# Attention's second stage in a hybrid decoder trunk: shares sent a step earlier, a merge over fewer steps, residual loads spread out, and a reordered end

## The chip, the cores and the metric

One NeuronCore of a Trainium2 chip runs the whole program. The metric is the device time of one execution in microseconds (us). Engines are named as in the profile: PE is TensorE's matmul, PEld its weight load, DVE is VectorE, ACT is ScalarE, POOL is GpSimd, SP is SyncE, which only issues DMAs here.

## The reference, cut to what matters

Two layers work on x of 1024 tokens by 1024 channels in float32: first a gated short convolution, then an attention layer. The change is in the attention layer:

```
h = rms_norm(x, attn_norm)
proj = h @ w_in                                 # q, k, v for 3 groups of 16 heads, and a gate z
for g, (window, dilation) in enumerate(((128, 1), (512, 4), (2048, 16))):
    q, k = rms_norm(...), rms_norm(...)
    out[g], lse[g] = dilated_group_attention(q, k, v, bias, window, dilation)
alpha = softmax(stack(lse), axis=0)             # a share for each of the 3 groups
o = sum(alpha * out)                            # merged per head and token
x = x + (o * silu(z)) @ w_out
```

## The kernel before, in words

Everything up to the projections q, k, v and z comes before the part that changes; it leaves q and k (`qkd`), v (`vd`), z (`zd`) and the residual stream (`x1d`) in HBM. The second stage of attention follows, from about 1626 us of the span to its end. The program fixes the order of every engine's instructions there by hand: PE, DVE, ACT, POOL and SP (the DMA queue) each run strictly in the order in which the code emits them.

**Units and steps.** The heads come in 8 pairs (`hp`, two heads side by side on 128 partitions) with 3 groups each. Groups 0 and 1 make 4 steps, group 2 makes 2, so a pair has 10 steps and the stage 80, numbered 0 to 79. A step's work is a dictionary from a lag to functions: what stands at lag n is emitted n steps after the step's own number. Lag 0 is A (L877): logits on PE, the row maximum on DVE (L899), the exponential on ACT (L902). Lag `LB` = 2 is B (L904): PE transposes the probabilities, DVE or ACT copies them out of PSUM. Lag `LC` = 4 is C (L913): PE multiplies with V, and `finish` (L935) copies a full bank into O on DVE. Within one step the lags are emitted in the order 0, 1, 4, 3, 5 to 14, 2 (L1143), then the products in `extra`, then the loads and splits in `begins`.

**The merge of a pair.** The maxima and sums of groups 0 and 1 are stored to `nld` by POOL (L947, L950) one step after the last step of their group. After the pair's last step `end` (number 10 hp + 9) come, at the lags of L1052: `store` at 1 reads them back as `ml` (POOL, L945); `weights` at 3 and `shares` at 4 compute the three shares in small tiles (DVE, one ACT exponential); `store_shares` at 4 writes them to `fd` (POOL, L980); `spread(w)` (L982) reads them back, broadcast over 64 partitions, in two DMAs of 256 KB for each w, into `fb`, a pool of two tiles; `scale(w)` (DVE, L988) multiplies O of group w; `add(w)` (POOL, L991) sums; `gate` at 12 (DVE, L994) multiplies with silu(z); `high` at 13 (ACT, L998) and `low` at 14 (DVE, L1001) split the result into two float32r parts, `y2`. The third share's `spread(0)` stands at lag 8, behind `scale(2)`, because its tile is the one that `scale(2)` frees.

**Beside it.** The output product is made in three rounds of two pairs, one (128 x 512) tile a step (`some`, L1096: 6 matmuls of 512 columns), from step 10(2r + 2) + `LD` on, `LD` = 14; `add_sums` (L1102) adds a finished tile to the residual `acc` on DVE at the start of the next step. Its weights are split on ACT and DVE four and three steps ahead. The residual tiles `acc` are read from `x1d` by 16 loads of 256 KB on SP, one a step from step 4 on (L1123). The last pair is merged without HBM: `wide` (L1003) widens the shares in SBUF, `spread_last` (L1014) transposes them into PSUM on PE, and `last` (L1023) does the rest half by half, between the last products. `sqacc` (L85) is a (128 x 1024) tile of an earlier stage that this stage doesn't use.

Of the kernel before, what the change touches and what calls it, by code (L numbers as in the profile page):

```python
# [19 lines left out]
P = 128  # L20
# [15 lines left out]
def trunk(ctx: ExitStack, tc: tile.TileContext, a, out):  # L36
# [776 lines left out]
    with tc.tile_pool(name="sp", bufs=3, space=PSUM) as sp, tc.tile_pool(name="ptp", bufs=2, space=PSUM) as ptp, \  # L813
# [37 lines left out]
        def attention(hp, g):  # L851
# [128 lines left out]
                nc.gpsimd.dma_start(fd[hp].rearrange("w s (i r) -> i w s r", r=8), u["fo"])  # L980

            def spread(w):  # L982
                fb = u["fb", w] = fbp.tile([P, S], F32, name="fb", tag="fb")
                for s, hs in enumerate((lo, up)):
                    nc.gpsimd.dma_start(fb[hs], fd[hp, w, s][None, :].to_broadcast([64, S]))

            def scale(w):
                nc.vector.tensor_tensor(O[hp, w], O[hp, w], u["fb", w], op=OP.mult)  # L988

            def add(w):  # L990
                nc.gpsimd.tensor_tensor(O[hp, 1], O[hp, 1], O[hp, w], op=OP.add)  # L991
# [22 lines left out]
            def spread_last(hf):  # L1014

                hs = slice(64 * hf, 64 * hf + 64)
                for w in (2, 1, 0):
                    fb = u["fb", w] = sp.tile([P, 4, P], F32, name="ps", tag="ps").rearrange("p a b -> p (a b)")
                    for r in range(8):
                        nc.tensor.transpose(fb.rearrange("p (i r) -> p r i", r=8)[:, r],  # L1020
                                            u["wide", w][hs, r * P:r * P + P], ident[hs, hs])

            def last(hf, i):  # L1023
                h, z = half(hf), SZ[hp][:, half(hf)]
                if i == 0:
                    for w in (2, 1, 0):
                        nc.vector.tensor_tensor(O[hp, w][:, h], O[hp, w][:, h], u["fb", w], op=OP.mult)
                elif i == 1:
                    for w in (2, 0):
                        nc.vector.tensor_tensor(O[hp, 1][:, h], O[hp, 1][:, h], O[hp, w][:, h], op=OP.add)  # L1030
                    nc.vector.tensor_tensor(z, O[hp, 1][:, h], z, op=OP.mult)
                    if hf == 0:
                        y2[hp] = [ap.tile([P, S], F32R, name="qk", tag="qk", bufs=6) for _ in range(2)]
                    nc.scalar.activation(y2[hp][0][:, h], z, AF.Copy)
                else:
                    nc.vector.tensor_tensor(y2[hp][1][:, h], z, y2[hp][0][:, h].bitcast(F32), op=OP.subtract)
# [5 lines left out]
                    st = make(js, not steps)  # L1042
                    steps.append({lag: [f] for lag, f in zip((0, LB, LC), st)})
            end = steps[-1]
            end.setdefault(1, []).append(store)
            if g == 2:
                if hp == HP - 1:
                    todo = [(LB, weights), (3, shares), (3, wide), (LC, lambda: spread_last(0)),
                            (LC, lambda: last(0, 0)), (LC, lambda: last(0, 1))]
                    ending.update(spread=spread_last, last=last)  # L1050
                else:
                    todo = [(3, weights), (LC, shares), (LC, store_shares), (LC, lambda: spread(2)),  # L1052
                            (LC, lambda: spread(1)), (8, lambda: scale(2)), (8, lambda: spread(0)),
                            (9, lambda: scale(1)), (9, lambda: add(2)), (11, lambda: scale(0)),
                            (11, lambda: add(0)), (12, gate), (13, high), (14, low)]
                for lag, f in todo:
                    end.setdefault(lag, []).append(f)
            return steps, prefetch

        LB, LC = 2, 4  # L1060
        LD = 14
        W, ending = {}, {}

        def dense(ps, kts, dt, hf, first, last):
# [55 lines left out]
        for un, (k, prefetch) in at.items():  # L1120
            when(max(0, k - 2), load_v, *un)
        for i, (dt, hf) in enumerate(tiles):
            when(4 + i, residual, dt, hf)  # L1123
        for r in range(3):
            k0 = at[2 * r + 2, 0][0] + LD
            k = k0
            for i, (dt, hf) in enumerate(tiles):
                late = k >= len(steps)
                name = "pd" if not late else ("pd", ("ps", "ps", "pt", "pt")[min(k - len(steps), 3)])[i % 2]
                extra.setdefault(k, []).append(lambda r=r, dt=dt, hf=hf, name=name:  # L1130
                                               some((2 * r, 2 * r + 1), dt, hf, name))
                k += i % 2 if late else 1
        for kt in range(KT):
            k = at[kt // 2 * 2 + 2, 0][0] + LD - 4 + kt % 2 if kt < 6 else len(steps) - 5 + kt % 2
            when(k - 4 - kt % 2, fetch, kt)
            when(k, split, kt)
            when(k + 1, split_low, kt)
        for f in begins.pop(-1):
            f()
        k = 0  # L1140
        while k < len(steps) + LC or any(x >= k for x in extra):
            add_sums()
            for lag in (0, 1, LC, 3, *range(LC + 1, 15), LB):  # L1143
                for f in steps[k - lag].get(lag, ()) if 0 <= k - lag < len(steps) else ():
                    f()
            for f in extra.get(k, ()):
                f()
            for f in begins.get(k, ()):
                f()
            k += 1  # L1150
# [94 lines left out]
```

## Time and profile before

| what | value |
|---|---|
| time before, median of 3 runs | 1992.55 us (1991.82 to 1994.5) |
| profiled execution: its own time | 1993.42 us |
| profiled execution: span of its instructions | 1991.5 us |
| PE busy | 1942.4 us, 98% of the span |
| DVE, ACT, POOL busy | 75%, 45%, 44% |
| mean granted TensorE clock | 0.994 of 2.4 GHz |

The profile lists single instructions with their start, length and the idle time of their engine just before them, and what ended that idle time. Busy PE time counts a matmul until its modelled end. A stretch's granted clock of 1.00 is 2.4 GHz, 0.50 is 1.2 GHz. "DMA share" is the mean busy share of the core's 16 DMA engines.

### The profile page before, as it was taken

The page shows a single profiled execution, that of the slowest core. Times are in us where ns is not written, and L with a number is a line of the kernel's source. Part 1 is how long each engine was busy: PE and PEld are TensorE (multiplying, and loading weights), DVE is VectorE, ACT ScalarE, POOL GpSimd, SP SyncE. Part 2 cuts the span into 40 slices and gives each one's busy share as a digit, 9 for nine tenths or more (in the row PEclk, how much of TensorE's full clock was granted, in tenths as well). Part 3 has the DMA queues.
Part 4 walks back from the last instruction along what each step waited for, and adds up shares of the span by engine and source line. Part 5 has one row for each costly group of instructions (what it writes and reads, how often), then busy time and mean ns, then how long its engine had stood idle before and what let it go on. Part 6 is the DMA issues. An engine that isn't in the chain of part 4 may idle for free.

```text
span 1991.5 us, 29494 instructions
## 1 busy us (share of the span) xinstructions
PE 1942.4 (98%) x10302; PEld 1579.2 (79%) x10302; DVE 1484.1 (75%) x2751; ACT 903.5 (45%) x2042; POOL 885.3 (44%) x800
## 2 busy tenths in 40 slices
PE   8999999999999999999999999999999998899998
PEld 6888888888887888788887888788888876677776
DVE  6866665666666555898888788878899856787886
ACT  6433333333335344534343434343443448777770
POOL 0356767667665112444455444544454442222330
PEclk9999999999999999999999999999999999999999
DMA  6313232232225565323333323332433278767752
GB/s 198 113 62 96 71 106 85 85 106 70 89 77 176 165 235 171 118 85 106 106 106 117 96 96 117 107 105 85 127 99 106 93 239 259 206 174 219 207 142 85
DMA packets 116805, 254.25 MB, mean 128 GB/s; under 512 B 15822, under 2 KB 22718, under 8 KB 116656
## 3 DMA queue, kind: packets, MB, share of 16 engines
q1 hardware_dynamic: 93024, 177.42, 28.4%
q0 software_dynamic: 23632, 74.95, 12.5%
q8 instruction: 81, 1.33, 0.3%
q14 instruction: 68, 0.56, 0.1%
HBM read 193.05 MB, written 67.64 MB: 131 GB/s over the span
## 4 chain that ended last, share of the span: by engine, by line
PE 77%; DVE 10%; issue 5%; DMA 4%; ACT 2%; POOL 1%; SPq 0%; DVEq 0%; POOLq 0%; ACTq 0%
PE pp L301 18%; PE pp L304 18%; PE pp L303 18%; PE pp L552 3%; PE pp L553 3%; PE pp L551 3%; DVE ws L165 2%; PE pt L909 2%; PE ps L891 2%; DMA nld<-nl 1%; DVE blkc L711 1%; PE pp L374 1%; PE pp L376 1%; PE pp L375 1%; PE po L928 1%
## 5 line engine op out<-in xcount | busy, mean ns | idle before, releaser
L165 DVE TENSOR_TENSOR ws<-wr,ws 128x512 fp32r<-128x512 f32 x284 | 265.3, 936 | 115.5 <-ACT ws L164 114.6
L164 ACT ACTIVATE ws<-wr 128x512 fp32r<-128x512 f32 x284 | 178.3, 629 | 360.4 <-PE pp L304 236.7
L276 POOL TENSOR_TENSOR sr<-wr 128x512 f32<-128x512 f32 x136 | 192.6, 1416 | 264.6 <-DMA wr<-in_conv_w_in 69.7
L164 ACT ACTIVATE ws<-sr 128x512 fp32r<-128x512 f32 x272 | 169.7, 629 | 285.5 <-PE pp L304 236.2
L165 DVE TENSOR_TENSOR ws<-sr,ws 128x512 fp32r<-128x512 f32 x272 | 227.6, 845 | 80.4 <-ACT ws L164 77.6
L313 DVE TENSOR_TENSOR f<-pp,f 128x512 f32<-128x512 f32 x204 | 139.5, 684 | 90.2 <-PE pp L304 83.3
L902 ACT ACTIVATE xs<-xs,nl 128x128 f32<-128x128 f32 (+1 forms) x384 | 167.9, 439 | 68.9 <-DVE nl L899 57.7
L309 ACT ACTIVATE f<-pp 128x512 f32<-128x512 f32 x228 | 132.7, 582 | 28.4 <-POOL blkc L683 14.5
L899 DVE CUSTOM_DVE_ANT_0 xs<-ps,bt 128x128 f32<-128x128 f32 (+1 forms) x384 | 110.9, 347 | 27.5 <-PE ps L891 16.3
L716 POOL DMA_DIRECT2D qkd<-blkc x96 | 68.1, 717 | 131.6 <-DVE blkc L711 123.0
L674 ACT ACTIVATE f<-f 128x512 f32<-128x512 f32 x96 | 60.7, 633 | 140.2 <-DVE f L313 103.1
L276 POOL TENSOR_TENSOR sr<-wr,sr 128x512 f32<-128x512 f32 x68 | 88.9, 1307 | 65.7 <-issue 43.4
L301 PE MATMUL pp<-blkg,ws 128*128 128x512 f32 x272 | 107.3, 394 | 4.3 <-ACT f L309 4.2
L301 PE MATMUL pp<-blkf,ws 128*128 128x512 f32 x272 | 108.5, 399 | 0.7 <-ACT f L309 0.7
L301 PE MATMUL pp<-blka,ws 128*128 128x512 f32 x272 | 107.1, 394 | 0.7 <-ACT f L309 0.7
L301 PE MATMUL pp<-blkb,ws 128*128 128x512 f32 x272 | 107.4, 395 | 0.0
L301 PE MATMUL pp<-blkd,ws 128*128 128x512 f32 x272 | 107.0, 393 | 0.0
L304 PE MATMUL pp<-blkf,ws 128*128 128x512 f32 x272 | 106.3, 391 | 0.0
L304 PE MATMUL pp<-blkd,ws 128*128 128x512 f32 x272 | 106.0, 390 | 0.0
L304 PE MATMUL pp<-blka,ws 128*128 128x512 f32 x272 | 106.0, 390 | 0.0
L304 PE MATMUL pp<-blkb,ws 128*128 128x512 f32 x272 | 106.0, 390 | 0.0
L301 PE MATMUL pp<-blke,ws 128*128 128x512 f32 x272 | 106.0, 390 | 0.0
(329 smaller groups left out, 5388.0 us busy)
## 6 DMA issues: line engine op xcount, KB each, us to landing
wr<-in_conv_w_in SPq DMA_DIRECT2D x128, 256.0 KB, 3.0
wr<-in_wqk SPq DMA_DIRECT2D x96, 256.0 KB, 3.1
qkd<-blkc POOLq DMA_DIRECT2D x96, 256.0 KB, 3.1
qk<-qkd SPq DMA_DIRECT2D x48, 512.0 KB, 8.6
wr<-in_conv_w_out SPq DMA_DIRECT2D x64, 256.0 KB, 3.1
f<-in_x SPq DMA_DIRECT2D x48, 256.0 KB, 4.3
wr<-in_wv SPq DMA_DIRECT2D x48, 256.0 KB, 3.0
vd<-f POOLq DMA_DIRECT2D x48, 256.0 KB, 2.5
```

Source lines behind the costliest of these rows:

```text
L164: nc.scalar.activation(t[:, 0], src, AF.Copy)
L165: nc.vector.tensor_tensor(t[:, 1], src, t[:, 0].bitcast(F32), op=OP.subtract)
L276: nc.gpsimd.tensor_tensor(t, x, y, op=op)
L301: nc.tensor.matmul(ps, w[:, 0, ws], b[:, k, 0], start=new and k == 0, stop=False, skip_group_check=not new)
L303: nc.tensor.matmul(ps, w[:, 0, ws], b[:, k, 1], start=False, stop=False, skip_group_check=not new)
L304: nc.tensor.matmul(ps, w[:, 1, ws], b[:, k, 0], start=False, stop=end and k == 3, skip_group_check=not new)
L309: nc.scalar.activation(t, ps, AF.Copy)
L313: nc.vector.tensor_tensor(m, ps, m, op=OP.add)
L674: nc.scalar.activation(sq, t, AF.Square)
L716: nc.gpsimd.dma_start(qkd[hp, g, which].rearrange("p (c s) -> p c s", c=c) [:, :, hf * m:(hf + 1) * m], o.rearrange("p (c s) -> p c s", c=c))
L899: nc.vector.tensor_tensor_reduce(out=x, in0=ps[s][:, x0:x0 + nk].rearrange("p a b -> p (a b)"), in1=u["bt"][s][:, bs], op0=OP.add, op1=OP. ...
L902: nc.scalar.activation(x, x, AF.Exp, bias=nm, scale=-1.0, accum_out=L)
```

## The change

`spread(0)` writes into `sqacc` instead of a third tile from the pool of two, and with `store_shares` and the other two spreads it is emitted at lag 3, with `shares`; `store` of group 2 moves from lag 1 to 0, `weights` from 3 to 2 (at the end of that step), `scale(0)` and `add(0)` from 11 to 10, `high` from 13 to 12, `low` from 14 to 13. `LD` becomes 13, so every round of output products, and the splitting of its weights, starts one step earlier. The residual loads stand at every second step from 6 to 36. In the last pair, C of its last two steps comes one step earlier, B of the last step and `weights` move to the end of step 80, the steps behind it follow one step sooner, and the last products of the third round are spread over other PSUM banks and one step less.

```diff
--- before.py
+++ after.py
@@ -980,7 +980,7 @@
                 nc.gpsimd.dma_start(fd[hp].rearrange("w s (i r) -> i w s r", r=8), u["fo"])
 
             def spread(w):
-                fb = u["fb", w] = fbp.tile([P, S], F32, name="fb", tag="fb")
+                fb = u["fb", w] = fbp.tile([P, S], F32, name="fb", tag="fb") if w else sqacc
                 for s, hs in enumerate((lo, up)):
                     nc.gpsimd.dma_start(fb[hs], fd[hp, w, s][None, :].to_broadcast([64, S]))
 
@@ -1042,23 +1042,25 @@
                     st = make(js, not steps)
                     steps.append({lag: [f] for lag, f in zip((0, LB, LC), st)})
             end = steps[-1]
-            end.setdefault(1, []).append(store)
+            end.setdefault(0 if g == 2 else 1, []).append(store)
             if g == 2:
                 if hp == HP - 1:
-                    todo = [(LB, weights), (3, shares), (3, wide), (LC, lambda: spread_last(0)),
-                            (LC, lambda: last(0, 0)), (LC, lambda: last(0, 1))]
-                    ending.update(spread=spread_last, last=last)
+                    steps[-2][3] = steps[-2].pop(LC)
+                    end[3] = end.pop(LC)
+                    todo = [(2, shares), (2, wide), (3, lambda: spread_last(0)), (3, lambda: last(0, 0)),
+                            (3, lambda: last(0, 1))]
+                    ending.update(turn=end.pop(LB)[0], weights=weights, spread=spread_last, last=last)
                 else:
-                    todo = [(3, weights), (LC, shares), (LC, store_shares), (LC, lambda: spread(2)),
-                            (LC, lambda: spread(1)), (8, lambda: scale(2)), (8, lambda: spread(0)),
-                            (9, lambda: scale(1)), (9, lambda: add(2)), (11, lambda: scale(0)),
-                            (11, lambda: add(0)), (12, gate), (13, high), (14, low)]
+                    todo = [(LB, weights), (3, shares), (3, store_shares), (3, lambda: spread(2)),
+                            (3, lambda: spread(1)), (3, lambda: spread(0)), (8, lambda: scale(2)),
+                            (9, lambda: scale(1)), (9, lambda: add(2)), (10, lambda: scale(0)),
+                            (10, lambda: add(0)), (12, gate), (12, high), (13, low)]
                 for lag, f in todo:
                     end.setdefault(lag, []).append(f)
             return steps, prefetch
 
         LB, LC = 2, 4
-        LD = 14
+        LD = 13
         W, ending = {}, {}
 
         def dense(ps, kts, dt, hf, first, last):
@@ -1120,25 +1122,30 @@
         for un, (k, prefetch) in at.items():
             when(max(0, k - 2), load_v, *un)
         for i, (dt, hf) in enumerate(tiles):
-            when(4 + i, residual, dt, hf)
+            when(6 + 2 * i, residual, dt, hf)
         for r in range(3):
             k0 = at[2 * r + 2, 0][0] + LD
             k = k0
             for i, (dt, hf) in enumerate(tiles):
                 late = k >= len(steps)
-                name = "pd" if not late else ("pd", ("ps", "ps", "pt", "pt")[min(k - len(steps), 3)])[i % 2]
+                name = "pd" if not late else (("pd", "ps"), ("pd", "ps"), ("pd", "pt"), ("pt", "pd"))[
+                    min(k - len(steps), 3)][i % 2]
+                if i >= 14:
+                    name = "po"
                 extra.setdefault(k, []).append(lambda r=r, dt=dt, hf=hf, name=name:
                                                some((2 * r, 2 * r + 1), dt, hf, name))
-                k += i % 2 if late else 1
+                k += (i % 2 if i < 13 else 0) if late else 1
         for kt in range(KT):
             k = at[kt // 2 * 2 + 2, 0][0] + LD - 4 + kt % 2 if kt < 6 else len(steps) - 5 + kt % 2
             when(k - 4 - kt % 2, fetch, kt)
             when(k, split, kt)
             when(k + 1, split_low, kt)
+        when(len(steps), ending["turn"])
+        when(len(steps), ending["weights"])
         for f in begins.pop(-1):
             f()
         k = 0
-        while k < len(steps) + LC or any(x >= k for x in extra):
+        while k < len(steps) + LC - 1 or any(x >= k for x in extra):
             add_sums()
             for lag in (0, 1, LC, 3, *range(LC + 1, 15), LB):
                 for f in steps[k - lag].get(lag, ()) if 0 <= k - lag < len(steps) else ():
```

## Rows read from the trace of the kernel before

**Rows 1.** Busy times by stretch, one head pair each, the last from step 80 on.

```profile
core 0: us, PE busy (x) PEld busy (x) DVE busy (x) ACT busy (x) POOL busy (x), PEclk, DMA share, GB/s
1655.92:1692.25 36.33, 31.20 (x342) 24.46 (x340) 24.02 (x119) 29.32 (x119) 9.37 (x12) 0.91 0.92 280
1692.25:1729.59 37.34, 31.66 (x340) 24.00 (x338) 27.10 (x122) 28.94 (x113) 11.74 (x13) 0.94 0.73 196
1729.59:1770.11 40.52, 38.94 (x378) 29.77 (x378) 33.28 (x131) 32.16 (x120) 11.75 (x13) 0.97 0.81 230
...
1812.20:1853.02 40.82, 37.65 (x378) 28.60 (x377) 33.19 (x130) 31.20 (x116) 11.74 (x13) 1.00 0.73 191
...
1895.12:1934.98 39.86, 38.12 (x366) 29.45 (x362) 34.43 (x131) 31.17 (x110) 12.26 (x14) 0.96 0.55 158
1934.98:1991.50 56.52, 48.26 (x317) 38.39 (x316) 35.74 (x61) 7.67 (x18) 2.38 (x1) 0.97 0.21 76
```

**Rows 2.** Waits of the stage: engine, line, cause, us in total, times, longest.

```profile
DVE o L988 <- DMA fb<-fd: 16.4, 10, 4.1
...
DVE sz L994 <- POOL o L991: 5.1, 6, 1.9
```

**Rows 3.** Timeline of DVE, 1676 to 1698 us: start, us, what, idle before.

```profile
1683.87 1.23 DVE L988 TENSOR_TENSOR o<-o,fb 128x1024 f32<-128x1024 f32 x1 [4.08 <-DMA fb<-fd]
```

**Rows 4.** Timeline of PE, 1680 to 1697 us.

```profile
1685.99 2.07 PE L891 MATMUL ps<-qk 64*128 64x128 f32 x14 [3.90 <-DVE nl L899]
```

**Rows 5.** Busy times by stretch: after that idle time, columns as in Rows 1.

```profile
1684.50:1691.30 6.80, 5.18 (x32) 4.23 (x32) 6.23 (x36) 5.54 (x27) 4.95 (x5) 0.50 1.05 293
```

**Rows 6.** Timeline of POOL, 1785 to 1822 us, merge of the fifth pair.

```profile
1790.73 2.10 POOL L985 DMA_DIRECT2D fb<-fd  x4 [2.31 <-DMA fd<-fo]
...
1803.66 1.05 POOL L985 DMA_DIRECT2D fb<-fd  x2 [9.93 <-DVE o L988]
1804.69 1.56 POOL L950 DMA_DIRECT2D nld<-nl  x2
...
1817.14 0.57 POOL L945 DMA_DIRECT2D ml<-nld  x1 [7.53 <-DVE o L988]
1817.72 2.38 POOL L991 TENSOR_TENSOR o<-o 128x1024 f32<-128x1024 f32 x1
```

**Rows 7.** DMA issues of the whole run: count, KB each, median us to landing.

```profile
fb<-fd POOLq DMA_DIRECT2D x42, 256.0 KB, 8.3
...
acc<-x1d SPq DMA_DIRECT2D x16, 256.0 KB, 7.2
...
nld<-nl POOLq DMA_DIRECT2D x16, 8.0 KB, 10.2
...
fd<-fo POOLq DMA_DIRECT2D x7, 24.0 KB, 3.0
```

**Rows 8.** Timeline of DVE, 1810 to 1831 us, same merge.

```profile
1815.60 1.23 DVE L988 TENSOR_TENSOR o<-o,fb 128x1024 f32<-128x1024 f32 x1 [2.20 <-DMA fb<-fd]
...
1820.13 1.22 DVE L994 TENSOR_TENSOR sz<-o,sz 128x1024 f32<-128x1024 f32 x1 [0.72 <-POOL o L991]
```

**Rows 9.** Groups by line, 1640 to 1992 us: busy us, mean ns.

```profile
L939 DVE COPY o<-po 128x512 f32<-128x512 f32 x48 | 32.2, 685 | 1.1 <-PE po L922 0.4 <-PE po L928 0.3
```

**Rows 10.** Timeline of PE, 1949 to 1970 us, near the end.

```profile
1957.86 0.79 PE L1069 MATMUL pd<-y,y 128*128 128x512 f32 x1 [2.34 <-DVE acc L1105]
1958.45 0.63 PE L1070 MATMUL pd<-y,y 128*128 128x512 f32 x1
...
1960.99 0.39 PE L1070 MATMUL pt<-y,y 128*128 128x512 f32 x1
```

**Rows 11.** Timeline, 1586 to 1588.2 us, DVE beside POOL, an earlier stage.

```profile
1586.62 1.29 POOL L276 TENSOR_TENSOR sr<-wr 128x512 f32<-128x512 f32 x1 [2.48 <-DMA wr<-in_wz]
1586.74 1.26 DVE L65 TENSOR_TENSOR rit<-ri 128x64 f32<-128x64 f32 x1
```

**Rows 12.** Instructions of line 65: ns minimum, median, maximum.

```profile
L65 DVE TENSOR_TENSOR rit<-ri x72: 209/226/1341, 857.5 to 1586.7; 128x64 f32<-128x64 f32 x72
```

## Prediction

> **What bounds the kernel now.** I read the span cut by head pair first. Where output products run in most steps PE has next to no idle time; the loss sits elsewhere. Of the second pair's 36.33 us PE is busy 31.20, of the third's 37.34 it is busy 31.66, of the sixth's 40.82 it is busy 37.65, of the eighth's 39.86 it is busy 38.12, and of the end's 56.52 it is busy 48.26, part of the rest being the last adds and the stores behind the last matmul [rows 1]. Its granted clock is below 1.00 in four of these five as well, so some of the busy time is work at 1.2 GHz.
>
> The list of waits says why. DVE stands 16.4 us before `scale` for the broadcast shares, in ten waits of up to 4.1, and 5.1 us before `gate` for POOL's `add` [rows 2]. DVE's order is fixed, so the next step's row maxima stand behind such a wait: in the merge of the first pair DVE waits 4.08 us, and PE is idle 3.90 us for exactly those maxima [rows 3, 4]. After that idle time the granted clock is 0.50 (1.2 GHz) for 6.80 us, in which PE is busy 5.18 [rows 5]. At 2.4 GHz that work is 2.6 us, so 2.6 us is the clock's part.
>
> POOL's timeline of a merge shows two chains. The first four share loads are issued at 1790.73; the last two stand 9.93 us until `scale(2)` frees a tile and go out at 1803.66, and `scale(0)` waits 2.20 us for them [rows 6, 8]. Behind these two stand the stores of the next pair's maxima (1804.69); `ml` waits for their landing until 1817.14, `add(0)` stands behind `ml`, and `gate` waits 0.72 us for `add(0)` [rows 6, 8]. Seven merges go this way.
>
> **The change, part by part.** The sum is made against the profiled execution's own 1993.42 us (span 1991.5 and 1.9 around it), 0.87 over the median of 1992.55.
>
> *Shares a step earlier, the third with them.* No DMA and no instruction is added. `scale(2)` and `scale(1)` stay where they are, so their loads gain one step: 36.33/10 = 3.6 us in the second pair, 37.34/10 = 3.7 in the third [rows 1]. The largest wait, 4.08, leaves 0.5. The third pair of loads now goes out in the same burst, some four steps earlier, while `scale(0)` moves up by one, so its wait goes. The cost is a burst of six instead of four; two more loads are 0.52 MB, 1.8 us at the 293 GB/s that a full stretch moved [rows 5, 7], behind the others. POOL is passed by nothing but its own DMAs, and the maxima's stores no longer stand behind a wait.
>
> What can be won is bounded by the next engine. *Second pair:* PE's work at full clock is 31.20 - 2.6 = 28.6 us, ACT's 29.32. The DMA engines moved 280 GB/s, 10.2 MB; five residual loads of 256 KB fewer fall here, leaving 8.9 MB, 30.3 us at 293 GB/s. So at most 36.3 - 30.3 = 6.0. I take 4.5, since at such a share of the DMA engines the loads land late: lower end 1. *Third pair:* a clock of 0.94 means 4.5 us at half speed, so PE's work is 31.66 - 2.2 = 29.5 and the most is 7.8. Five residual loads are added, 7.3 + 1.3 MB, 29.4 us: the DMA engines come up to PE. I take 4.5, lower end 1. *Fourth pair:* 1.58 idle and 1.2 for the clock (0.97), most 2.8, taken 1.5. *Sixth:* 3.17 idle, taken 1.5. *Eighth:* 1.74 idle and 1.6 for the clock (0.96), most 3.3, taken 1.5 [rows 1]. About half, because there DVE is next: with `LD` one less the splits of two weight rows, `gate`, `weights` and `shares` fall on four neighbouring steps that have no output product to cover them. Lower ends 0. The fifth and seventh pairs have no PE idle time and give nothing.
>
> *`LD` = 13 and the residual loads.* The products move as a block; their number per round and the adds are the same. Cost nothing by themselves: PE has no idle time while they run. The 16 residual loads take no engine's time; they land in 7.2 us [rows 7] and the first is wanted 27 steps after it is issued. If their cover went, the price is the DMA time counted above.
>
> *The end.* The last product tiles wait 2.34 us for a bank whose add stands behind the merge of the first half on DVE, and then start at 1.2 GHz: 0.79 and 0.63 us a matmul where 0.39 is normal [rows 10]. A clock of 0.97 over 56.52 us is 3.4 us at half speed, 1.7 lost [rows 1]. The change gives the last tiles other banks and moves the merge up a step: most 4.0. It also puts C of steps 77 and 78 next to each other, and the second needs the bank that the first's copy (0.685 us [rows 9]) frees, behind a small `weights` on DVE: I take 1.2 for it and 0.3 for what is left of the wait, so 2.5 is won; lower end 0.
>
> *New costs.* `high` now stands in the same step as `gate` and ahead of ACT's copies of that step, so ACT stands until `gate` (1.22 us [rows 8]) is done; before, a step lay between. And `add(0)` on POOL (2.38 us [rows 6]) now runs while DVE reaches the split of a weight row in three merges. A DVE operation with both inputs in SBUF that meets a POOL operation ends with it: 1.26 us beside POOL's 1.29, where the median of that line is 0.226 [rows 11, 12]. Together they cost between 0 and 7.1 (three times 2.38); I take 2.0, because a step's maxima lie between `scale(0)` and the split and use up most of `add(0)`.
>
> The Trainium skill has this as a rule against the change (SBUF — State Buffer, "Who interferes with whom"): a VectorE operation with two SBUF inputs and a GpSimd operation that reads SBUF contend, and whoever comes second is blocked. The trace agrees, with the two rows just named. Taken at its full length three times it would make the sum 16.0 - 7.1 = 8.9 won instead of 14.0.
>
> *Sum:* 4.5 + 4.5 + 1.5 + 1.5 + 1.5 + 2.5 = 16.0, less 2.0: 14.0 us. 1993.42 - 14.0 = 1979.4 for an execution like the profiled one, 1978.6 beside the median; I say **1979.0**. The ends of the terms: 27.1 at most, and 2 less 7.1, a loss of 5, at the other end.
>
> **The rivals.** *More is won.* If the DMA engines keep up and the half-speed stretches all go, about 25 of the 27.1 us come: 1967.5. For it: each half-speed stretch in the stage stands behind idle time of the kind that the change removes [rows 4, 5]. Against it: the DMA share of the second pair is 0.92 [rows 1].
>
> *The DMA engines become the bound.* In 6.80 us of the first merge their share was 1.05 [rows 5]. If the six loads and the store of the shares (3.0 us [rows 7]) land as much later as they go out earlier, the second and third pairs give 1 each instead of 9, and 14 - 7 = 7 is left: 1985.5. For it: these are the pairs that lose most and have the fullest queues, and the third gets more loads. Against it: the second gets fewer.
>
> *Slower: one chain, stores of the maxima, `ml`, `add(0)`, `gate`, and now `high`.* The landing (10.2 us [rows 7]) holds `ml`, `ml` holds `add(0)` on POOL, `gate` waits on DVE, and with `high` behind it ACT now stands too. `gate` does not move up, but the steps before it get shorter. Priced at the longest wait of now, 1.9, and 1.22 for ACT, a merge loses 3.1, seven lose 21.8, against 16.0 won: 1992.55 + 5.8 = 1998.4. It decides above 2.3 us a merge. Against it: the stores are freed from the two loads ahead of them, which went out only at 1803.66 [rows 6].
>
> *It does not do what it says.* `ml` is emitted a step earlier, but its issue is held by the landing, not by its place. If `weights` now waits for it, the shares leave no sooner and only the third share's wait goes, which DVE loses again at `weights`: about 1992.
>
> **How the numbers follow.** A change of 0.2%, 4.0 us, is about what a measurement of this kernel can tell from none. Forecast 0.62 (its own range 1973 to 1985), more won 0.14, DMA engines 0.14, not as said 0.05, slower 0.05. The range 1969 to 1989 leaves out half of the second case and the last two: 0.17. Faster by more than 0.2%: the first three less a little for the third, 0.88; within 0.2%: 0.06; slower: 0.06.
>
> **What would show it.** Right: the second and third pairs take 31 to 33 us each, with a clock of at least 0.97; waits of `scale` for shares fall from 16.4 to under 4; no share load waits for `scale(2)`; the 2.34 us at the end shrinks to under 1 and a wait of about 1 appears before C of step 78. Wrong: waits before `gate` or `weights` in the place of those before `scale`; ACT idle between its exponentials and `high`; a DMA share near 1 with shares still landing late; or a gain in the fifth and seventh pairs, which I put at nothing.

## The result, and the profile after

The changed kernel takes 1983.18 us (median of 4 executions, 1981.16 to 1983.32) against 1992.44 us (4, 1991.82 to 1994.5) of the kernel before: 9.3 us won, ratio 0.9949 [0.9932, 0.9967]. Forecast was 1979.0, in a range of 1969 to 1989. The profiled execution after took 1981.16 us (span 1979.4), 2.0 under its median, and the one before 0.98 over its own. So the two traces differ by 12.1 us of span, of which some 3 us are scatter between executions; whatever is read from the traces alone adds up to 12.1, not 9.3. One execution in this document is an outlier, 4950.88 us in the last run (e11): its median below is that of all five, its ratio that of the other four.

The busy times by stretch of the changed kernel, one row for each head pair from the first, the last row from step 79 on, answer to [rows 1]:

```profile
core 0: us, PE busy (x) PEld busy (x) DVE busy (x) ACT busy (x) POOL busy (x), PEclk, DMA share, GB/s
1626.89:1654.91 28.02, 23.80 (x230) 17.02 (x230) 18.13 (x103) 25.87 (x101) 4.11 (x5) 1.00 0.71 250
1654.91:1686.66 31.75, 29.35 (x354) 23.04 (x351) 25.30 (x120) 29.52 (x121) 9.24 (x12) 1.00 0.90 250
1686.66:1722.71 36.05, 31.39 (x348) 23.72 (x348) 27.32 (x123) 30.22 (x116) 11.65 (x13) 1.00 0.88 233
1722.71:1764.95 42.24, 39.99 (x362) 30.69 (x364) 35.59 (x132) 31.03 (x115) 12.55 (x15) 0.92 0.94 275
1764.95:1806.44 41.49, 41.41 (x406) 31.94 (x402) 33.27 (x133) 28.77 (x112) 11.24 (x13) 1.00 0.70 208
1806.44:1846.58 40.14, 37.84 (x372) 28.90 (x374) 34.37 (x133) 31.64 (x119) 11.14 (x13) 1.00 0.72 191
1846.58:1888.07 41.49, 41.41 (x406) 31.94 (x402) 33.30 (x133) 28.78 (x113) 12.14 (x14) 1.00 0.71 204
1888.07:1924.72 36.65, 34.35 (x344) 26.30 (x345) 32.37 (x115) 29.78 (x102) 9.72 (x12) 1.00 0.52 150
1924.72:1979.40 54.68, 47.27 (x324) 38.33 (x323) 37.51 (x77) 9.42 (x27) 4.24 (x3) 1.00 0.21 78
```

[Rows 1] cut the end at step 80. The change reorders work inside step 79, so here both kernels are cut at its start. The same view of the kernel before, for the stretches that [rows 1] left out or cut otherwise:

```profile
1626.84:1655.92 29.08, 25.20 (x230) 18.22 (x230) 18.12 (x103) 26.11 (x101) 4.12 (x5) 0.94 0.78 266
1770.11:1812.20 42.09, 42.09 (x402) 32.49 (x400) 33.90 (x132) 29.38 (x114) 11.77 (x13) 1.00 0.72 202
1853.02:1895.12 42.10, 42.10 (x402) 32.50 (x401) 34.03 (x133) 29.39 (x114) 11.78 (x13) 1.00 0.70 191
1895.12:1932.92 37.80, 36.06 (x356) 28.01 (x352) 32.37 (x115) 29.45 (x101) 10.41 (x13) 0.95 0.58 166
1932.92:1991.50 58.58, 50.32 (x328) 39.83 (x326) 37.80 (x78) 9.39 (x27) 4.24 (x3) 0.97 0.20 73
```

The lengths can't be subtracted as they stand. `LD` = 13 moves the block of products by one step across the cuts, and a product tile has six matmuls that start 0.23 us apart, 1.4 us. Each of a round's two head pairs adds three matmuls to a tile. The same view for the first of the three counts the tiles (two such matmuls to a tile), after and then before, for pairs four and five:

```profile
1722.71:1764.95 42.24, 6.10 (x14) 2.64 (x14) 0.92 0.94 275
1764.95:1806.44 41.49, 7.85 (x18) 3.40 (x18) 1.00 0.70 208
```

```profile
1729.59:1770.11 40.52, 5.23 (x12) 2.27 (x12) 0.97 0.81 230
1770.11:1812.20 42.09, 8.72 (x20) 3.77 (x20) 1.00 0.72 202
```

One tile more in the fourth pair, one less in the fifth; likewise more in the sixth and eighth, less in the seventh and the end. With 1.4 us for it, the stretches changed by:

| stretch | before | after | change, tiles evened out | predicted |
|---|---|---|---|---|
| first pair | 29.08 | 28.02 | -1.1 | 0 |
| second | 36.33 | 31.75 | -4.6 | -4.5 |
| third | 37.34 | 36.05 | -1.3 | -4.5 |
| fourth | 40.52 | 42.24 | +0.3 | -1.5 |
| fifth and seventh | 42.1 each | 41.49 each | +0.8 each | 0 |
| sixth | 40.82 | 40.14 | -2.1 | -1.5 |
| eighth, to step 78 | 37.80 | 36.65 | -2.5 | -1.5 |
| from step 79 | 58.58 | 54.68 | -2.5 | -2.5 |

Most of what these changes add up to is work done at the higher clock: over these rows PE's busy time falls from 335.2 to 326.8 us for the same matmuls, its idle time only from 29.4 to 25.7. At a granted clock of 0.50 stood 23.9 us of the stage before (3.4 in the first pair, 6.8 in the second, 6.9 in the third, 3.4 each in the eighth and at the end), and 6.8 us after, all in the fourth pair.

The list of waits of the stage after has no row any more for `scale` behind a share (16.4 us in [rows 2]) nor for `gate` behind `add` (5.1 us). What DVE and ACT wait for in their place (us in total, times, longest):

```profile
ACT y L998 <- DVE sz L994: 4.9, 5, 2.1
...
ACT y L1082 <- DMA wraw<-in_wo: 2.6, 1, 2.6
DVE xs L899 <- DMA nld<-nl: 2.6, 1, 2.6
...
DVE mx L959 <- DMA ml<-nld: 2.2, 2, 1.7
```

[Rows 6] calls the merge that runs in the fifth pair's steps the fifth pair's; by the step of its loads (43) it is the fourth pair's. In POOL's timeline of the same merge after, six share loads go out in one go, with the store of the next maxima right behind them; the stand of 9.93 us of [rows 6] is gone:

```profile
1779.37 2.09 POOL L985 DMA_DIRECT2D fb<-fd  x4 [1.88 <-DMA fd<-fo]
1781.44 1.05 POOL L985 DMA_DIRECT2D sqacc<-fd  x2
1782.45 0.94 POOL L947 DMA_DIRECT2D nld<-nl  x1
```

The DMA issues of the stage after (count, KB each, median us to landing) show what the burst does to the landings; `fb` stood at 8.3 in [rows 7]:

```profile
fb<-fd POOLq DMA_DIRECT2D x28, 256.0 KB, 8.9
...
wraw<-in_wo SPq DMA_DIRECT2D x8, 512.0 KB, 17.4
...
sqacc<-fd POOLq DMA_DIRECT2D x14, 256.0 KB, 14.1
...
nld<-nl POOLq DMA_DIRECT2D x16, 8.0 KB, 8.7
...
nld<-nl POOLq DMA_DIRECT2D x8, 16.0 KB, 15.7
```

The 16 KB rows are the maxima and sums of group 0. They stand right behind the burst, which is six loads now and was four. Before, the same view had:

```profile
nld<-nl POOLq DMA_DIRECT2D x8, 16.0 KB, 11.1
```

Where the third pair ends, two of these late landings stop the engines in this execution. The store issued at 1704.79 lands 17.7 us later; the tile of maxima that it reads is one of three (`bufs=3` in `begin`) and is the one that step 30's row maxima write. DVE's timeline there, with a split that took 2.78 us where this line's median is 1.22, beside POOL's `add(0)` at 1724.16 (2.37 us):

```profile
1718.87 1.21 DVE L988 TENSOR_TENSOR o<-o,sqacc 128x1024 f32<-128x1024 f32 x1
1722.71 0.29 DVE L899 CUSTOM_DVE_ANT_0 xs<-ps,bt 128x128 f32<-128x128 f32 x1 [2.62 <-DMA nld<-nl]
...
1724.84 2.78 DVE L1085 TENSOR_TENSOR y<-wraw,y 128x1024 fp32r<-128x1024 f32 x1 [0.33 <-ACT y L1082]
```

ACT's timeline has the other: the weight row issued at 1703.59 landed at 1723.64, 20.1 us later.

```profile
1723.75 1.06 ACT L1082 ACTIVATE y<-wraw 128x1024 fp32r<-128x1024 f32 x1 [2.65 <-DMA wraw<-in_wo]
```

Behind these waits come two stretches of 3.4 us at a granted clock of 0.50, from 1723.5 and from 1733.7; they are the 0.92 of the fourth pair. Near the end PE's timeline has, in the place of 2.34 us and two slow matmuls [rows 10], three shorter stops at full clock. The first is the predicted wait for C of step 78; the third isn't new, it stood there with 1.15 us before the change as well:

```profile
1934.05 1.15 PE L922 MATMUL po<-pts,V 128*64 128x64 f32 x30 [0.69 <-DVE o L939]
...
1946.20 0.50 PE L1071 MATMUL pd<-y,y 128*128 128x512 f32 x1 [0.98 <-DVE acc L1107]
...
1957.20 0.50 PE L1072 MATMUL pt<-qk,y 128*128 128x512 f32 x1 [1.15 <-DVE qk L1036]
```

### The profile page after: what moved, and what is told of

It reads as the page before. It is cut to its first block, busy times and chain, and to the rows that moved or that the text cites. A ratio compares the mean times of both kernels' runs of the same rounds, so it can differ in the third digit from the quotient of the medians.

```text
span 1979.4 us, 29520 instructions
## 1 busy us (share of the span) xinstructions
PE 1934.5 (98%) x10302; PEld 1573.3 (79%) x10302; DVE 1486.2 (75%) x2751; ACT 902.5 (46%) x2042; POOL 882.9 (45%) x800
## 4 chain that ended last, share of the span: by engine, by line
PE 79%; DVE 12%; issue 4%; ACT 3%; DMA 1%; POOL 0%; SPq 0%; DVEq 0%; ACTq 0%; POOLq 0%
PE pp L301 18%; PE pp L304 18%; PE pp L303 18%; PE pp L551 3%; PE pp L553 3%; PE pp L552 3%; DVE ws L165 2%; PE pt L909 2%; PE ps L891 2%; PE po L928 2%; ACT xs L902 2%; DVE blkc L711 1%; PE pp L374 1%; PE pp L375 1%; PE pp L376 1%
## 5 line engine op out<-in xcount | busy, mean ns | idle before, releaser
L301 PE MATMUL pp<-blkb,ws 128*128 128x512 f32 x272 | 108.0, 397 | 0.0
L301 PE MATMUL pp<-blka,ws 128*128 128x512 f32 x272 | 107.1, 394 | 0.7 <-ACT f L309 0.7
L276 POOL TENSOR_TENSOR sr<-sr,wr 128x512 f32<-128x512 f32 x68 | 104.6, 1538 | 4.9
L304 PE MATMUL pp<-blkb,ws 128*128 128x512 f32 x272 | 106.7, 392 | 0.0
L303 PE MATMUL pp<-blkb,ws 128*128 128x512 f32 x272 | 106.5, 391 | 0.0
```

Of the source, the lines that this page charges most:

```text
L276: nc.gpsimd.tensor_tensor(t, x, y, op=op)
L301: nc.tensor.matmul(ps, w[:, 0, ws], b[:, k, 0], start=new and k == 0, stop=False, skip_group_check=not new)
L303: nc.tensor.matmul(ps, w[:, 0, ws], b[:, k, 1], start=False, stop=False, skip_group_check=not new)
L304: nc.tensor.matmul(ps, w[:, 1, ws], b[:, k, 0], start=False, stop=end and k == 3, skip_group_check=not new)
```

## The experiments

All times are medians, the ratios against the kernel before on the same chip (1992.1 to 1992.9 us there); e1 to e8, e10 and e11 start from the changed kernel. Lengths of pairs are those of one profiled execution each.

**The residual loads.** Put back to one a step:

```diff
-            when(6 + 2 * i, residual, dt, hf)
+            when(4 + i, residual, dt, hf)
```

> The changed kernel with the 16 residual loads back at one a step from step 4. Theory (late landings): the changed kernel gained only 1.3 us in the third pair and nothing in the fourth because DMAs land late there: a weight row in 20.1 us (ACT stands 2.65 us for it), the maxima's store in 17.7 us (DVE stands 2.62 us for its tile), and two half-speed stretches follow. With the residual loads early, both waits shrink by half or more and the third and fourth pairs get 2 to 4 us shorter, while steps 0 to 9 lose the 1.1 us and the second pair 1 to 2 us: in all -1 to +1 us against the changed kernel's 1983.2. Rival (the spreading itself is the gain of the first two pairs): the second pair loses 3 or more and the third wins nothing, 1986 or more.

1983.27 us, 0.9951 [0.9934, 0.9967]. The second pair takes 33.37 us (1.6 more), the third 34.40 (1.6 less), and the two waits of 2.6 us above are gone. In this execution the spread loads give in one pair what they take in the next; e10, which has the loads one a step too, takes 32.30 and 35.54 us there, so the sizes aren't settled.

**The tile of maxima.** Three more buffers:

```diff
-                u["nl"] = sm.tile([P, 8, 4], F32, name="nl", tag="nl", bufs=3)
+                u["nl"] = sm.tile([P, 8, 4], F32, name="nl", tag="nl", bufs=6)
```

> The changed kernel with six tiles instead of three for the maxima and sums (nl), so that no new unit waits for an old unit's store to land. Theory (two landings that hide one another): DVE's 2.62 us before step 30 go, but ACT stands for the weight row until about the same moment, so only 0 to 1 us is won: 1982.2 to 1983.2. Rival (DVE's wait alone is the stop): 2.6 us or more won, under 1980.6.

1982.37 us, 0.9953 [0.9935, 0.997]. By the busy times of its third and fourth pairs, the third is 3.4 us shorter than in the changed kernel, and the fourth has its full clock:

```profile
1687.18:1719.84 32.66, 29.11 (x338) 22.29 (x338) 27.20 (x123) 29.04 (x114) 11.67 (x13) 1.00 0.90 245
1719.84:1762.44 42.60, 38.58 (x371) 29.31 (x372) 35.27 (x132) 32.11 (x119) 12.56 (x15) 1.00 0.98 285
```

DVE's stop at that tile is gone, and it is gone in every run below with six tiles. But 3.4 us isn't shown to be its price, because other landings are late in other executions of the same steps. e7 has this run's program up to step 40, and its third pair takes 35.36 us, with `scale` waiting for shares again:

```profile
1714.78 1.22 DVE L988 TENSOR_TENSOR o<-o,fb 128x1024 f32<-128x1024 f32 x1 [0.82 <-DMA fb<-fd]
...
1723.55 1.22 DVE L988 TENSOR_TENSOR o<-o,sqacc 128x1024 f32<-128x1024 f32 x1 [1.57 <-DMA sqacc<-fd]
```

And with three tiles the stop shows up in the changed kernel's profiled execution only: e1, e3, e5 and e10 don't have it, and their third pairs take 34.3 to 35.5 us. The fourth pair stays long even at full clock, with a DMA share of 0.98; the medians (0.8 us apart) don't tell the two kernels apart.

**`high` behind the step's B.** ACT's copy then stands behind the evictions and isn't met by `gate`:

```diff
-                            (10, lambda: add(0)), (12, gate), (12, high), (13, low)]
+                            (10, lambda: add(0)), (12, gate), (15, high), (13, low)]
...
                 for f in steps[k - lag].get(lag, ()) if 0 <= k - lag < len(steps) else ():
                     f()
+            for f in steps[k - 12].get(15, ()) if 0 <= k - 12 < len(steps) else ():
+                f()
```

> The changed kernel with high emitted behind B's copies of the same step instead of ahead of them. Theory (ACT's stand behind gate costs, my step on new costs): ACT's 4.9 us of waits for gate go, PE's idle times of 1.55, 1.49 and 1.49 us before B in the fourth, sixth and eighth pairs shrink to under 0.7, and 2 to 3 us are won: 1980 to 1981. Rival (DVE's own work bounds these steps, 4.78 us busy of 4.85): PE idles as long, for DVE, and the time stays within 1 us of 1983.2.

1983.18 us, 0.9954 [0.9938, 0.997]. ACT's waits for `gate` are gone (in their place it waits 3.3 us in all for DVE's part of `weights`), and PE's idle time there, in the sixth pair, falls from 1.49 us to 0.55 and 0.37. Yet the sixth and eighth pairs take 40.13 and 36.67 us, as before the edit: ACT's stand costs nothing while DVE is the later of the two.

**Weight rows loaded sooner.** The six tiles of maxima, and two steps more for the loads:

```diff
-            when(k - 4 - kt % 2, fetch, kt)
+            when(k - (6 if kt < 6 else 4) - kt % 2, fetch, kt)
```

> Both landings taken out of the way: six nl tiles, and the weight rows of the first three rounds fetched two steps earlier. Theory (late landings): both waits of about 2.6 us before step 30 go, the half-speed stretch behind them too, and the third and fourth pairs together get 4 to 6 us shorter: 1977 to 1979. Rival (DVE's and ACT's own work bounds these steps): under 1.5 us won.

1985.53 us, 0.9963 [0.995, 0.9976]. It missed on all sides: the third pair takes 40.05 us, 4.0 more than in the changed kernel, clear of the 32.7 to 36.1 us of the other runs with this order. The weight rows land in time, but the query and key loads behind them don't, as PE's timeline shows:

```profile
1718.78 1.91 PE L909 MATMUL pt<-ident,xs 128*128 128x128 f32 x8 [1.07 <-DVE pts L847]
1725.70 1.65 PE L891 MATMUL ps<-qk 64*128 64x128 f32 x8 [5.02 <-DMA qk<-qkd]
```

**The end as before,** with `LD` = 13 kept:

```diff
-                    steps[-2][3] = steps[-2].pop(LC)
-                    end[3] = end.pop(LC)
-                    todo = [(2, shares), (2, wide), (3, lambda: spread_last(0)), (3, lambda: last(0, 0)),
-                            (3, lambda: last(0, 1))]
+                    todo = [(LB, weights), (3, shares), (3, wide), (LC, lambda: spread_last(0)),
+                            (LC, lambda: last(0, 0)), (LC, lambda: last(0, 1))]
...
-                k += (i % 2 if i < 13 else 0) if late else 1
+                k += i % 2 if late else 1
```

The banks of the last products (not shown) are as before too.

> The changed kernel with the end as before: the last pair's old lags, old banks and old spacing of the last products; LD stays 13. Measured on the stretch from step 79 to the end: 58.63 us before, 54.67 with the change, of which 1.4 is one product tile that LD moved out of it. Theory (my step on the end): the wait of about 2.3 us for a bank comes back and the stretch takes 56.5 to 57.5 us, 2 to 3 us longer than with the change. Rival (PE is bound there and only the granted clock differed): 54.7 to 55.5 at full clock.

1982.81 us, 0.9954 [0.9941, 0.9967], so undoing the end costs nothing that can be measured. Its end took 56.55 us in the profiled execution, 1.9 more than after, but with 3.4 us at half speed in it. In runs that keep the new end the same stretch takes 54.7 us without such a stretch (the changed kernel, e1, e2, e6, e7) and 56.2 to 56.4 with one (e3, e4, e8, e11). Like with like the reorder is worth about 0.3 us. The old end had the half-speed stretch in all four of its profiled executions (the kernel before, e5, e9, e10), the new one in four of nine; whether the reorder makes it rarer is open. In the place of the two bank waits of 0.69 and 0.98 us there is one, with `LD` = 13 already shorter than the 2.34 of [rows 10]:

```profile
1949.38 0.50 PE L1069 MATMUL pd<-y,y 128*128 128x512 f32 x1 [1.38 <-DVE acc L1105]
```

**The third share late again:** its own tile, its place and `scale(0)`, `add(0)` as before; the first two stay a step sooner.

```diff
-fb = u["fb", w] = fbp.tile([P, S], F32, name="fb", tag="fb") if w else sqacc
+fb = u["fb", w] = fbp.tile([P, S], F32, name="fb", tag="fb")
...
-(3, lambda: spread(1)), (3, lambda: spread(0)), (8, lambda: scale(2)),
+(3, lambda: spread(1)), (8, lambda: scale(2)), (8, lambda: spread(0)),
...
-(10, lambda: scale(0)),
-(10, lambda: add(0)),
+(11, lambda: scale(0)),
+(11, lambda: add(0)),
```

> The changed kernel with the third share as before: its own tile from the pool of two, spread(0) at lag 8 behind scale(2), scale(0) and add(0) at 11. The first two shares still go a step sooner. Theory (the third share is worth about as much as the step): scale(0) waits 0.5 to 2.5 us for its share again in most merges and gate waits for add(0), so the second, third, sixth and eighth pairs get 1 to 2 us longer; but the burst is four loads again, the maxima's store lands in about 11 us instead of 15 to 18, and the third pair loses its 2.62 us wait for it. In all +2 to +5 us: 1985 to 1988. Rival (the step alone is the gain, the third share is hidden either way): within 1 us of 1983.2 or faster, by the third pair's 2.62.

1992.76 us, 1.0003 [0.9991, 1.0014]: the whole gain is gone, more than was expected by any reading. Its list of waits has POOL's load issue behind `scale(2)` again and shares late again, although the first two are sent as early as in the changed kernel:

```profile
POOL fb L985 <- DVE o L988: 70.6, 5, 15.8
...
DVE o L988 <- DMA fb<-fd: 9.9, 5, 4.4
...
DVE sz L994 <- POOL o L991: 2.2, 2, 1.3
```

What stands behind that issue on POOL is late with it. In the merge of the fourth pair the stores of the next maxima go out at 1804.33, and `ml` only after their landing:

```profile
1803.30 1.04 POOL L985 DMA_DIRECT2D fb<-fd  x2 [15.77 <-DVE o L988]
1804.33 1.56 POOL L950 DMA_DIRECT2D nld<-nl  x2
...
1814.65 0.57 POOL L945 DMA_DIRECT2D ml<-nld  x1 [5.40 <-issue]
```

`weights` then waits for `ml`, and step 51, in which it stands, takes 7.5 us in place of 4.9. The loss isn't everywhere, though: the second pair takes 30.4 us here, less than in the changed kernel (some 1 us of it because `scale(0)` stands behind the cut), and the third 36.6. It is the fourth, sixth and eighth, with the splits of the weight rows, that lose 3.8 to 4.6 us each.

**The third share alone:** the kernel before with only this edit.

```diff
-fb = u["fb", w] = fbp.tile([P, S], F32, name="fb", tag="fb")
+fb = u["fb", w] = fbp.tile([P, S], F32, name="fb", tag="fb") if w else sqacc
...
-(LC, lambda: spread(1)), (8, lambda: scale(2)), (8, lambda: spread(0)),
+(LC, lambda: spread(1)), (LC, lambda: spread(0)), (8, lambda: scale(2)),
```

> The kernel before with one part of the change alone: spread(0) goes into sqacc and is emitted at lag 4 with the other two; nothing is moved a step earlier, scale(0) stays at 11. Theory (the third share's place is nearly the whole gain, as its removal from the changed kernel brought 1992.8): scale(0) waits no more, gate waits less, the second and third pairs keep their waits for the first shares (about 3 us together) and in all 5 to 8 us are won: 1984 to 1987. Rival (only the step and the third share together win, because the first shares' waits of 4.08 and 2.50 us take its place): 0 to 3 us won, 1989 to 1992.

1987.57 us, 0.9975 [0.9964, 0.9986]: 4.9 us (2.8 to 7.2 by the interval), about half of the gain, just under what was expected. The waits before `gate` are gone from its list, and those for shares fall from 16.4 us to:

```profile
DVE o L988 <- DMA fb<-fd: 6.8, 4, 2.4
```

By stretch it wins where e6 loses. The second pair gives only 0.9 us, the third 2.2, the fourth 2.4 (with the same number of product tiles as before), the sixth 2.8:

```profile
1657.61:1693.00 35.39, 31.70 (x358) 24.94 (x354) 23.93 (x119) 30.53 (x122) 9.32 (x12) 0.95 0.92 272
1693.00:1728.12 35.12, 31.09 (x339) 24.02 (x337) 27.00 (x123) 29.00 (x114) 11.64 (x13) 0.95 0.82 223
1728.12:1766.28 38.16, 37.08 (x368) 28.07 (x369) 33.08 (x131) 31.14 (x116) 11.65 (x13) 1.00 0.84 226
...
1808.01:1846.03 38.02, 37.15 (x378) 28.58 (x377) 33.11 (x131) 31.11 (x116) 11.08 (x12) 1.00 0.78 214
```

This profiled execution was one of its fastest (1984.91 of 1983.8 to 1991.54).

**The merge alone:** residual loads (as in e1) and the end (as in e5) undone together.

> The changed kernel with both the residual loads and the end as before, so that only the merge part and LD of 13 are left. Theory (the residual loads and the reordered end are worth nothing that shows): within 2 us of 1983.2. Rival (each hides the other's worth): 1986 or more.

1985.12 us, 0.9961 [0.9947, 0.9975]: 7.3 of the 9.3 us. With e1 and e5 this leaves some 2 us, which the intervals don't tell from nothing, for the other two parts together. What it has beyond e9 is the earlier step and `LD` = 13: 2.4 us by the medians, with intervals that overlap. In the profiled executions the stage, from the first pair's start to the end, takes 354.0 us here and 354.2 in e9. `LD` = 13 by itself was not tested.

**Splits away from `gate`.** Six tiles of maxima, and the weight rows of the second and third round loaded and split four steps sooner:

```diff
+            k -= 4 if kt in (2, 3, 4, 5) else 0
             when(k - 4 - kt % 2, fetch, kt)
             when(k, split, kt)
```

> The changed kernel with six nl tiles, and the weight rows of the second and third round fetched and split four steps earlier, in steps 45, 46, 65 and 66, where DVE is busy 2.3 to 2.5 us of 4.1 to 4.5. Theory (DVE's own work bounds the four steps without products in the sixth and eighth pairs, and POOL's add stretches a split there from 1.22 to 1.65 us): PE's 2.4 us of idle time in each of the two pairs fall under 1, the sixth and eighth pairs get 1 to 2 us shorter than 40.1 and 36.7, and the third pair stays at the 32.7 us that six tiles gave: 1976 to 1979 in all. Rival (ACT or the DMAs hold these steps as much as DVE): the two pairs stay within 0.5 us.

1979.59 us, 0.9944 [0.9932, 0.9957]. The sixth and eighth pairs take 38.96 and 35.50 us, 1.2 less each, well clear of scatter: 40.1 to 40.2 and 36.7 in all of the changed kernel, e1 to e5 and e10. The fifth and seventh take 42.05 each, 0.56 more. The rest of the expectation missed: PE's idle time in each of the two pairs is 1.4 us, not under 1, the third pair's 35.36 us are not 32.7, and the time is just above the range. The splits moved from pairs in which DVE is late to pairs in which PE is busy throughout: DVE's load about `gate`, and the lock of split and `add(0)` with it, were part of the sixth's and eighth's length.

**Both:** e7 with `high` behind B as in e3.

> As the run before, and high behind B's copies of its step. Theory (once DVE's splits are gone, ACT's stand behind gate is next): another 0.5 to 1 us less in each of the fourth, sixth and eighth pairs, 1974 to 1978 in all. Rival (gate's place on DVE is what B waits for, whichever engine copies): no difference to the run before.

1979.24 us, 0.9937 [0.9923, 0.995], the shortest of all, but above the expected 1974 to 1978; its interval overlaps that of the changed kernel. With DVE relieved, `high`'s place now is worth 0.5 us in the sixth and eighth pairs, and nothing in the fourth (43.65 us, ACT waiting 2.58 for the weight row):

```profile
1806.45:1844.86 38.41, 37.39 (x371) 28.94 (x373) 31.71 (x130) 30.02 (x117) 11.98 (x14) 1.00 0.76 212
...
1886.91:1921.87 34.96, 33.94 (x344) 26.33 (x345) 29.71 (x113) 28.20 (x101) 9.70 (x12) 1.00 0.44 126
```

**Residual loads with a hole,** on e8, so that none falls into the merge that runs in the third pair's steps:

```diff
-            when(6 + 2 * i, residual, dt, hf)
+            when(4 + 2 * i if i < 8 else 23 + i, residual, dt, hf)
```

> Run e8 (six nl tiles, four weight rows split earlier, high behind B's copies) with no residual load in steps 19 to 30: eight at every second step from 4 to 18, eight from step 31 to 38. Theory (the DMA engines are what still holds the third pair and the head of the fourth: ACT stands 2.58 us for a weight row there): that wait falls under 1, no share lands late, the third pair takes 31.5 to 33 us and the fourth 41 to 42, 1975 to 1977 in all. Rival (the queue of six share loads alone delays the weight row): the two pairs stay at 33.6 and 43.7 us, 1979.

1981.13 us, 0.9942 [0.9927, 0.9956]. The weight row's wait is gone and the fourth pair is 41.63 us, but the third is 35.05 (33.59 in e8): `scale(0)` now waits 1.68 us for its share and `weights` 1.52 us for `ml`. Another landing is late, and no time is won. That the hole made it late isn't shown: e7 waits as long for its shares without it.

## Why the prediction was right, and where not

**The mechanism held.** No share load waits for `scale(2)`, the waits for shares and before `gate` went to nothing in this profile (in the other runs with this order up to 2.9 us for shares are left in all, and at most 2.1 in one wait), and the second pair's 31.75 us are the 31 to 33 forecast, at full clock: 4.6 us against 4.5. The sixth pair gave 2.1 against 1.5. The eighth gave 2.5 against 1.5, part of it the half-speed stretch that stood behind its clock of 0.96 [rows 1]. Some 0.8 us of either only crossed a cut, as said below. That POOL's in-order queue was the lever is shown by e6 and e9: without the third share's early place nothing is left; with it alone, about half. The second pair is the exception: its gain is the earlier step, as the sum had it, since it is there without the third share's place (30.4 us in e6) and hardly there with that alone (35.39 in e9). The rest of the merge's 7.3 us, as far as the medians show it, takes the earlier step and `LD` = 13 as well.

**The step that failed is "third pair 4.5, fourth 1.5".** They gave 1.3, and lost 0.3. I took the burst of six as 1.8 us more DMA time behind the four loads and said that the stores of the maxima no longer stand behind a wait. They don't, but one of them stands behind the burst: 17.7 us to landing. I named `ml` as who waits for them, and not the row maxima three units on, which reuse the tile that the store reads. With six tiles that stop is gone, and in e2 the third pair is 32.66 us, inside the forecast. But four runs with three tiles don't have the stop either, and in e7, with six, late shares make the pair 35.36. So the error is wider than one tile: at the end of the third pair something lands 1 to 3 us late, now the store, now a share, now the weight row on SP's queue (ACT's 2.65 us in the fourth pair, with half-speed stretches behind it), and which one differs between executions. e4 and e11 moved loads, and each time another wait stood in the place of the one removed. That is the rival "the DMA engines become the bound" at work in these two pairs, not as a share of 1 throughout, but as landings of 15 to 20 us. The burst by itself isn't enough for it: e9 has the same burst a step later, with the product rounds a step later as well, and wins 4.6 us in these two pairs; the profiled executions with the new order give 1.0 (the changed kernel) to 4.0 (e2) in the two together, against 6.0 forecast, but for e4, which loses. What makes the difference to e9 stays open. I also counted five residual loads into the third pair and not the four that fall into the fourth; e1 and e10, without those four, take 42.55 and 40.71 us there, so nothing shows them to be the cause.

**The end** came out at 2.5 us as forecast, for other reasons. e5 puts the reorder at about 0.3; the clock is 1.5 to 1.7 by the lengths above, and the remaining 0.6 or so is in e5 as well, so it came with `LD` or the merge. The predicted wait before C of step 78 came at 0.69 us (1.2 forecast), and the 2.34 us became 0.98, but they became 1.38 without the reorder too. The step that failed here is "the change gives the last tiles other banks and moves the merge up a step" as the source of the 2.5.

**The new costs** were sized well and placed partly wrong. The lock of [rows 11] came at each of the three splits: 2.78, 1.65 and 1.65 us in place of 1.22, 2.4 us in all where I took 2.0 with ACT's part. The Trainium skill's rule (SBUF — State Buffer, "Who interferes with whom": whichever of the two comes second is blocked) agrees with these rows. The 7.1 us of the prediction were not reached, since the split met only the tail of `add(0)` twice. ACT's stand before `high` was there (four times 0.6 to 0.8 us, and 2.1 in the last pair's steps), and e3 shows that it cost nothing by itself.

**Put at nothing:** the residual loads, rightly as far as e1's median shows; the fifth and seventh pairs lost 0.8 each, which I had excluded. In e6, with `LD` = 13 as well, both take 40.70 us, just one tile less than before, and in e9, with the third share's place but `scale(0)` at lag 11, 41.73 and 42.09 us, nothing more than before. So the 0.8 come with `scale(0)` at lag 10. They aren't time lost but work that crosses the cut: the changed kernel's DVE timeline has that `scale(0)` (1.22 us) at 1805.31, in step 49 and ahead of the sixth pair's first row maximum at 1806.44; in e6 it stands behind the cut. Taken in twos, fifth and sixth gave 1.3 us, seventh and eighth 1.7, against 1.5 each forecast. The first pair's 1.1 us is clock alone, and luck: 28.0 us in the changed kernel, e1, e2 and e6, 29.1 in the kernel before and all other runs, which have 3.4 us at half speed there.

**The other rivals.** The slower chain through `ml`, `add(0)` and `gate` didn't form: `weights` waited 2.2 us for `ml` in all and `gate` not at all. "More is won" failed at the third and fourth pairs. Its argument, that each half-speed stretch stands behind idle time that the change removes, does not hold for the first pair and the end, where the same stops are there with and without such a stretch.

## What to carry to other kernels

Look first for an issue that stands in an in-order queue because its tile isn't free: one more tile there was worth about half of this gain alone, and without it none was left, since what stood behind that issue was late as well. When a burst is moved forward, list every tile whose reuse waits for a landing of a transfer behind the burst, stores included, and not only those who read what is loaded. Before a wait of 2 to 3 us is priced from one trace, look whether it is there in the trace of another run that has the same program in those steps; here the wait moved from one landing to another. Read stretch by stretch with the work in each evened out: the totals hid a shortfall of 5 us in two pairs, and would have given an edit at the end credit for the clock.

## Not expected of the hardware

The same work and the same idle time before it is sometimes followed by a half-speed stretch and sometimes not. The first pair's steps, with the same work on PE, DVE and ACT in every kernel, and a stop of 2.2 us on PE in all of them, took 28.0 us in four runs and 29.1 in the others. The new end, with PE idle 0.80, 0.69, 0.98 and 1.15 us at the same places, took 54.7 in five runs and 56.2 to 56.4 in four, where the granted clock was 0.50 for 3.4 us from the last of these stops on. The four executions that spared the first pair spared the end too. Together that is some 2.6 us, a good part of the scatter of these kernels, and as much as several terms of the sum.

A load of 256 KB that lands in some 8 us in a full stretch lands in 14.1 us as the fifth and sixth of a burst, and a store of 16 KB behind it needs 15.7 us in the median: a transfer's time depended more on what stood in the queues than on its size.
